# A row mean over 512 MiB: the first tile loaded in four DMAs over strided partitions

## The chip, the cores and the metric

The kernel runs on one core of a Trainium2 chip, alone. The metric is the device time of one launch in microseconds; lower is better. The core has TensorE (PE), VectorE (DVE), ScalarE (ACT), GpSimd (POOL) and SyncE (SP), and 16 DMA engines that move data between HBM and the on-chip memory, SBUF. SBUF has 128 partitions; a tile has rows in partitions.

## The reference

```python
def setup_inputs():
    return {"x": np.random.randn(64, 256, 8192).astype(np.float32)}

def reference(x):
    return np.mean(x, axis=2)
```

The input is 64 x 256 = 16,384 rows of L = 8192 float32 numbers, 536.87 MB in all. Each row gives one number, its mean, so the output is 65.5 kB.

## The kernel before

The rows are taken in tiles of 256: partition p of a tile holds rows 2p and 2p + 1 of it, one after the other, so that it is 16,384 numbers, or 65,536 contiguous bytes of HBM, for each partition. `NP` = 63 tiles go this way (t = 0 to 62), and the last 256 rows go as two half tiles of 128 rows, one row to a partition; the second of these is cut into four column chunks, so that little work is left after the last bytes have landed.

Three buffers (`NBUF` = 3) of 128 x 16,384 float32 take the tiles in turn; tile t goes to buffer t mod 3. Each buffer has its own semaphore, `in_sems[t % NBUF]`, which a DMA raises by 16 when all of its parts have landed.

- SP issues all loads in order (`sync_program`, lines 91 to 101). From tile 3 on it first waits until VectorE has done the tile that was in the buffer before (`dve_sem`). After the loads it issues the three stores of the output.
- VectorE (`vector_program`) waits for a tile's semaphore and sums each of the two rows of each partition with one `tensor_reduce` (line 119). For tile t the semaphore has to stand at 16 for each tile that the buffer has taken, this one among them: `16 * (t // NBUF + 1)`.
- ScalarE (`scalar_program`) is idle until the end, where it shares the last full tile and the half tiles with VectorE (line 153).
- At the end TensorE transposes the sums, so that they can be stored as contiguous rows, and ScalarE scales them by 1/L. The very last 128 rows are summed up and transposed on VectorE (lines 143 to 147).
- GpSimd writes an identity matrix and zeros at the start (lines 76 to 79).

The order of work is written by hand, in each engine's program. One thing is done after that: the instructions of the first `NBUF` loads, which wait for nothing, are cut out of the program and put ahead of SP's first drain, which belongs to a barrier of all engines at the start (lines 192 to 200). SP thus issues these loads before it comes to the barrier. The code counts them: it takes the first `NBUF` instructions that follow the position `first`.

Of the kernel before, what the change touches and what calls it, by code (L numbers as in the profile page):

```python
# [6 lines left out]
def bass_global_avg_pool_1d_kernel(  # L7
# [4 lines left out]
    P = 128  # L12
# [13 lines left out]
    NP = rows // (R * P) - 1  # L26
    NBUF = 3
# [5 lines left out]
    x_pair = x_rows.rearrange("(t p r) l -> t p (r l)", p=P, r=R)  # L33
# [8 lines left out]
    with ExitStack() as ctx:  # L42
        E = ctx.enter_context
        bufs = [E(nc.sbuf_tensor(f"buf{i}", [P, R * L], f32)) for i in range(NBUF)]
        res = E(nc.sbuf_tensor("res", [P, NP, R], f32))
        res1 = E(nc.sbuf_tensor("res1", [P, 2], f32))
        part = E(nc.sbuf_tensor("part", [P, 8], f32))
        fin = E(nc.sbuf_tensor("fin", [P, 32], f32))
        fint = E(nc.sbuf_tensor("fint", [P, 32], f32))
        ident = E(nc.sbuf_tensor("ident", [P, P], f32))  # L50
        outsb = E(nc.sbuf_tensor("outsb", [NP, P, R], f32))
        out1sb = E(nc.sbuf_tensor("out1sb", [1, P], f32))
        ps = [E(nc.psum_tensor(f"ps{r}", [NP, P], f32)) for r in range(R)]
        psone = E(nc.psum_tensor("psone", [1, P], f32))

        in_sems = [E(nc.semaphore(f"in_sem{i}")) for i in range(NBUF)]
        one_sem = E(nc.semaphore("one_sem"))
        ch_sems = [E(nc.semaphore(f"ch_sem{i}")) for i in range(NCH)]
        dve_sem = E(nc.semaphore("dve_sem"))
        act_sem = E(nc.semaphore("act_sem"))  # L60
        prep_sem = E(nc.semaphore("prep_sem"))
        pe_sem = E(nc.semaphore("pe_sem"))
        cp_sem = E(nc.semaphore("cp_sem"))
        fin_sem = E(nc.semaphore("fin_sem"))
        out_sems = [E(nc.semaphore(f"out_sem{i}")) for i in range(3)]

        b1 = NP % NBUF
        b2 = (NP + 1) % NBUF
        buf1 = bufs[b1]
        buf2 = bufs[b2]  # L70
        offs = [sum(CH[:i]) for i in range(NCH)]
        s0 = CH[0] // 2 - L // 64
        s1 = CH[1] // 2

        def gpsimd_program(eng):
            eng.memset(fin[:], 0.0).then_inc(prep_sem, 1)  # L76
            eng.memset(ident[:], 0.0).then_inc(prep_sem, 1)  # L77
            eng.wait_ge(prep_sem, 2)
            eng.affine_select(  # L79
                out=ident[:],  # L80
                in_=ident[:],
                compare_op=mybir.AluOpType.not_equal,
                fill=1.0,
                base=0,
                pattern=[[-1, P]],
                channel_multiplier=1,
            ).then_inc(prep_sem, 1)

        first = len(nc.main_func.blocks[0].instructions)

        def sync_program(eng):
            for t in range(NP):
                if t >= NBUF:
                    eng.wait_ge(dve_sem, t - NBUF + 1)
                eng.dma_start(bufs[t % NBUF][:], x_pair[t]).then_inc(in_sems[t % NBUF], 16)  # L95
            eng.wait_ge(dve_sem, NP - NBUF + 1)
            eng.dma_start(buf1[:, :L], x_one[T1]).then_inc(one_sem, 16)
            eng.wait_ge(dve_sem, NP - NBUF + 2)
            for c in range(NCH):
                sl = slice(offs[c], offs[c] + CH[c])  # L100
                eng.dma_start(buf2[:, sl], x_one[T2][:, sl]).then_inc(ch_sems[c], 16)  # L101

            eng.wait_ge(cp_sem, 2)
            eng.dma_start(out_pair[0:NP, :], outsb[:].rearrange("t p r -> t (p r)")).then_inc(
                out_sems[0], 16
            )
            eng.wait_ge(cp_sem, 3)
            eng.dma_start(out_one[T1 : T1 + 1, :], out1sb[:]).then_inc(out_sems[1], 16)
            eng.wait_ge(fin_sem, 3)
            eng.dma_start(out_q[4 * T2 : 4 * T2 + 4, :], fint[0:P:32, :]).then_inc(  # L110
                out_sems[2], 16
            )
            for s in out_sems:
                eng.wait_ge(s, 16)

        def vector_program(eng):
            for t in range(NP - 1):
                eng.wait_ge(in_sems[t % NBUF], 16 * (t // NBUF + 1))
                eng.tensor_reduce(  # L119
                    res[:, t, :],  # L120
                    bufs[t % NBUF][:].rearrange("p (r l) -> p r l", r=R),
                    X,
                    ADD,
                ).then_inc(dve_sem, 1)
            t = NP - 1
            eng.wait_ge(in_sems[t % NBUF], 16 * (t // NBUF + 1))
            eng.tensor_reduce(res[:, t, 0:1], bufs[t % NBUF][:, :L], X, ADD).then_inc(dve_sem, 1)  # L127
            eng.wait_ge(one_sem, 16)
            eng.tensor_reduce(res1[:, 0:1], buf1[:, : L // 2], X, ADD).then_inc(dve_sem, 1)  # L129
            eng.wait_ge(ch_sems[0], 16)  # L130
            eng.tensor_reduce(part[:, 0:1], buf2[:, :s0], X, ADD).then_inc(dve_sem, 1)  # L131
            eng.wait_ge(ch_sems[1], 16)
            eng.tensor_reduce(  # L133
                part[:, 1:2], buf2[:, offs[1] : offs[1] + s1], X, ADD
            ).then_inc(dve_sem, 1)
            eng.wait_ge(ch_sems[3], 16)
            eng.tensor_reduce(  # L137
                part[:, 2:3], buf2[:, offs[3] : offs[3] + CH[3]], X, ADD
            ).then_inc(dve_sem, 1)
            eng.wait_ge(dve_sem, NP + 4)  # L140
            eng.wait_ge(act_sem, 5)
            eng.wait_ge(prep_sem, 1)
            eng.tensor_reduce(fin[:, 0:1], part[:, 0:6], X, ADD).then_inc(fin_sem, 1)  # L143
            eng.wait_ge(fin_sem, 1)
            eng.transpose(fint[:], fin[:]).then_inc(fin_sem, 1)  # L145
            eng.wait_ge(fin_sem, 2)
            eng.tensor_scalar(  # L147
                fint[:], fint[:], inv, None, mybir.AluOpType.mult
            ).then_inc(fin_sem, 1)

        def scalar_program(eng):
            def acc(dst, src):
                eng.activation(src, src, Copy, accum_out=dst).then_inc(act_sem, 1)  # L153

            t = NP - 1
            eng.wait_ge(in_sems[t % NBUF], 16 * (t // NBUF + 1))
            acc(res[:, t, 1:2], bufs[t % NBUF][:, L:])
            eng.wait_ge(one_sem, 16)
            acc(res1[:, 1:2], buf1[:, L // 2 : L])

            for r in range(R):
                eng.wait_ge(pe_sem, r + 1)
                eng.activation(outsb[:, :, r], ps[r][:], Copy, scale=inv).then_inc(cp_sem, 1)  # L163
            eng.wait_ge(pe_sem, 3)
            eng.activation(out1sb[:], psone[:], Copy, scale=inv).then_inc(cp_sem, 1)  # L165
            eng.wait_ge(ch_sems[0], 16)
            acc(part[:, 3:4], buf2[:, s0 : CH[0]])
            eng.wait_ge(ch_sems[1], 16)
            acc(part[:, 4:5], buf2[:, offs[1] + s1 : offs[1] + CH[1]])
            eng.wait_ge(ch_sems[2], 16)  # L170
            acc(part[:, 5:6], buf2[:, offs[2] : offs[2] + CH[2]])

        def tensor_program(eng):
            eng.wait_ge(prep_sem, 3)
            eng.wait_ge(dve_sem, NP)
            eng.wait_ge(act_sem, 1)
            for r in range(R):
                eng.transpose(ps[r][:], res[:, :, r], ident[:]).then_inc(pe_sem, 1)  # L178
            eng.wait_ge(dve_sem, NP + 1)
            eng.wait_ge(act_sem, 2)  # L180
            eng.matmul(psone[:], res1[:, 0:1], ident[:], start=True, stop=False)  # L181
            eng.matmul(psone[:], res1[:, 1:2], ident[:], start=False, stop=True).then_inc(pe_sem, 1)  # L182

        sync_program(nc.sync)
        gpsimd_program(nc.gpsimd)
        vector_program(nc.vector)
        scalar_program(nc.scalar)
        tensor_program(nc.tensor)

        stream = nc.main_func.blocks[0].instructions
        loads = stream[first : first + NBUF]
        del stream[first : first + NBUF]
        at = next(
            i
            for i, ins in enumerate(stream)
            if ins.engine == mybir.EngineType.SP and type(ins).__name__ == "InstDrain"
        )
        stream[at:at] = loads  # L200
# [28 lines left out]
```

## Time and profile before

| what | value |
|---|---|
| median of 3 runs | 1247.26 us (1247.18 to 1247.38) |
| the profiled execution | 1247.12 us |
| its span, from the first to the last instruction | 1245.3 us |
| VectorE busy | 1085.6 us, 87% |
| DMA queue q1, share of 16 engines' span | 99.7%, mean 431 GB/s |
| one `tensor_reduce` of a full tile (line 119) | 17.22 us |
| one issue of a load on SP (line 95) | 0.33 to 0.43 us |
| from a load's issue to its landing (line 95) | 21.9 us for the first, 40.8 us median |

The profile is one execution, recorded by the hardware. Times in its views are microseconds from the span's start, means of one instruction are in nanoseconds. A row of the timeline has its start, its duration, engine, line, operation, output and input, and in brackets the idle time of the engine before it with what ended that. "SPq" is SP's queue of DMA issues. The DMA row gives the busy share of the 16 DMA engines in tenths, slice by slice, and the row below it the rate in GB/s. The chain is the work that ended last, followed back from the last instruction. The trace also holds a record of every DMA packet, with its start, duration and bytes, from which single packets are told.

### The profile page before, as it was taken

To read this page: it belongs to the slowest core of one execution; us is meant where nothing else is said; L and a number is where in the kernel's file an instruction comes from. 1 tells how busy PE (TensorE), PEld (TensorE's weight loads), DVE (VectorE), ACT (ScalarE), POOL (GpSimd) and SP (SyncE) were. 2 spreads that over 40 slices of the span, in tenths; PEclk is the share of its full clock that TensorE was granted. 3 is DMA by queue.
4 is the path that set the end of the run, shared out by engine and by line. 5 is a ranking of instruction groups with operands and counts; after the bars stand their busy time and mean duration, and the time that the engine had idled before them with its cause. 6 is when DMAs were issued, how large, how long until landed. Compare 5 with 4: busy or idle time off the path is not lost.

```text
span 1245.3 us, 194 instructions
## 1 busy us (share of the span) xinstructions
PE 1.7 (0%) x6; PEld 0.6 (0%) x6; DVE 1085.6 (87%) x70; ACT 17.2 (1%) x14; POOL 0.8 (0%) x7
## 2 busy tenths in 40 slices
PE   0000000000000000000000000000000000000000
PEld 0000000000000000000000000000000000000000
DVE  2898988988889889898898988989889898898897
ACT  0000000000000000000000000000000000000005
POOL 0000000000000000000000000000000000000000
DMA  9999999999999999999999999999999999999998
GB/s 434 421 425 438 438 438 438 436 421 423 438 438 438 438 438 436 410 434 438 438 438 438 438 432 413 436 438 438 436 438 438 421 423 438 438 438 436 438 438 341
DMA packets 9876, 536.95 MB, mean 431 GB/s; under 512 B 1107, under 2 KB 1171, under 8 KB 1427
## 3 DMA queue, kind: packets, MB, share of 16 engines
q1 hardware_dynamic: 9874, 536.94, 99.7%
q14 instruction: 2, 0.01, 0.0%
HBM read 536.87 MB, written 0.07 MB: 431 GB/s over the span
## 4 chain that ended last, share of the span: by engine, by line
DMA 70%; DVE 29%; SPq 0%; issue 0%
DMA buf<-in_x_dram 70%; DVE res L119 29%; SPq L101 0%; DVE part L137 0%; SPq L95 0%; DVE fint L145 0%; DVE fint L147 0%; DVE fin L143 0%
## 5 line engine op out<-in xcount | busy, mean ns | idle before, releaser
L119 DVE TENSOR_REDUCE res<-buf 128x2 f32<-128x16384 f32 x62 | 1067.6, 17220 | 152.9 <-DMA buf<-in_x_dram 152.9
L153 ACT ACTIVATE buf<-buf 128x1024 f32<-128x1024 f32 (+3 forms) x5 | 15.0, 2994 | 1222.3 <-DMA buf<-in_x_dram 1222.2
L127 DVE TENSOR_REDUCE res<-buf 128x1 f32<-128x8192 f32 x1 | 8.7, 8686 | 2.1 <-DMA buf<-in_x_dram 2.1
L129 DVE TENSOR_REDUCE res<-buf 128x1 f32<-128x4096 f32 x1 | 4.4, 4420 | 1.0 <-DMA buf<-in_x_dram 1.0
L131 DVE TENSOR_REDUCE part<-buf 128x1 f32<-128x2176 f32 x1 | 2.4, 2419 | 1.1 <-DMA buf<-in_x_dram 1.1
L178 PE MATMUL ps<-ident,res 128*63 128x128 f32 x2 | 0.7, 430 | 1231.5 <-DVE res L127 1231.5
L153 ACT ACT_TABLE_LOAD x1 | 1.3, 1283 | 1.8 <-PEq L214 1.8
L133 DVE TENSOR_REDUCE part<-buf 128x1 f32<-128x1024 f32 x1 | 1.2, 1219 | 0.1
L137 DVE TENSOR_REDUCE part<-buf 128x1 f32<-128x512 f32 x1 | 0.7, 687 | 0.7 <-DMA buf<-in_x_dram 0.7
L153 ACT ACTIVATION_READ_ACCUMULATOR buf<-buf 128x1 f32 x5 | 0.9, 186 | 0.0
L178 PEld LDWEIGHTS ps<-ident,res 128*63 128x63 f32 x2 | 0.3, 205 | 1231.4 <-issue 1231.4
L182 PE MATMUL psone<-ident,res 128*1 128x128 f32 x2 | 0.6, 421 | 0.0
L181 PE MATMUL psone<-ident,res 128*1 128x128 f32 x2 | 0.6, 397 | 4.7 <-DVE res L129 4.7
L163 ACT ACTIVATE outsb<-ps 63x128 f32<-63x128 f32 x2 | 0.4, 264 | 0.0
L79 POOL TENSOR_SCALAR_AFFINE_SELECT ident<-ident 128x128 f32<-128x128 f32 x1 | 0.3, 292 | 0.2 <-POOL ident L77 0.2
L165 ACT ACTIVATE out1sb<-psone 1x128 f32<-1x128 f32 x1 | 0.3, 267 | 1.5 <-PE psone L182 1.5
L182 PEld LDWEIGHTS psone<-ident,res 128*1 128x1 f32 x2 | 0.3, 128 | 0.2
L145 DVE STREAM_TRANSPOSE fint<-fin 128x32 f32<-128x32 f32 x1 | 0.2, 212 | 0.0
L147 DVE TENSOR_SCALAR fint<-fint 128x32 f32<-128x32 f32 x1 | 0.2, 181 | 0.0
L77 POOL MEMSET ident<- 128x128 f32 x1 | 0.2, 204 | 0.0
L143 DVE TENSOR_REDUCE fin<-part 128x1 f32<-128x6 f32 x1 | 0.2, 158 | 0.0
L76 POOL MEMSET fin<- 128x32 f32 x1 | 0.1, 125 | 1.3 <-POOLq L214 1.3
(5 smaller groups left out, 0.5 us busy)
## 6 DMA issues: line engine op xcount, KB each, us to landing
buf<-in_x_dram SPq DMA_DIRECT2D x1, 4096.0 KB, 31.1
buf<-in_x_dram SPq DMA_DIRECT2D x1, 2304.0 KB, 17.3
buf<-in_x_dram SPq DMA_DIRECT2D x1, 1024.0 KB, 19.4
buf<-in_x_dram SPq DMA_DIRECT2D x63, 40.8
buf<-in_x_dram SPq DMA_DIRECT2D x1, 512.0 KB, 20.2
buf<-in_x_dram SPq DMA_DIRECT2D x1, 256.0 KB, 20.3
out_dram<-outsb SPq DMA_DIRECT2D x1, 63.0 KB
out_dram<-out1sb SPq DMA_DIRECT2D x1, 0.5 KB
```

Of the source, the lines that this page charges most:

```text
L79: eng.affine_select(out=ident[:], in_=ident[:], compare_op=mybir.AluOpType.not_equal, fill=1.0, base=0, pattern=[[-1, P]], channel_multipl ...
L119: eng.tensor_reduce(res[:, t, :], bufs[t % NBUF][:].rearrange("p (r l) -> p r l", r=R), X, ADD,).then_inc(dve_sem, 1)
L127: eng.tensor_reduce(res[:, t, 0:1], bufs[t % NBUF][:, :L], X, ADD).then_inc(dve_sem, 1)
L129: eng.tensor_reduce(res1[:, 0:1], buf1[:, : L // 2], X, ADD).then_inc(dve_sem, 1)
L131: eng.tensor_reduce(part[:, 0:1], buf2[:, :s0], X, ADD).then_inc(dve_sem, 1)
L133: eng.tensor_reduce(part[:, 1:2], buf2[:, offs[1] : offs[1] + s1], X, ADD).then_inc(dve_sem, 1)
L137: eng.tensor_reduce(part[:, 2:3], buf2[:, offs[3] : offs[3] + CH[3]], X, ADD).then_inc(dve_sem, 1)
L153: eng.activation(src, src, Copy, accum_out=dst).then_inc(act_sem, 1)
L163: eng.activation(outsb[:, :, r], ps[r][:], Copy, scale=inv).then_inc(cp_sem, 1)
L178: eng.transpose(ps[r][:], res[:, :, r], ident[:]).then_inc(pe_sem, 1)
L181: eng.matmul(psone[:], res1[:, 0:1], ident[:], start=True, stop=False)
L182: eng.matmul(psone[:], res1[:, 1:2], ident[:], start=False, stop=True).then_inc(pe_sem, 1)
```

## The change

The load of tile 0 is no longer one DMA over all 128 partitions. Four DMAs take its place, on the same queue and in this order: partitions 0, 8, 16, ... (16 of them), partitions 4, 12, 20, ... (16), partitions 2, 6, 10, ... (32) and the odd partitions (64). Each moves the same 65,536 bytes to each of its partitions as before, from the same place in HBM. All four raise the semaphore of buffer 0 by 16, so a new function `landed(t)` gives the count to wait for: 48 more than before for all tiles of buffer 0. The block of instructions that is moved ahead of SP's drain grows by three. All else is as it was.

```diff
+        def landed(t):
+            return 16 * (t // NBUF + 1 + 3 * (t % NBUF == 0))
+
...
         def sync_program(eng):
-            for t in range(NP):
+
+
+            for p, step in ((0, 8), (4, 8), (2, 4), (1, 2)):
+                eng.dma_start(bufs[0][p:P:step, :], x_pair[0][p:P:step, :]).then_inc(
+                    in_sems[0], 16
+                )
+            for t in range(1, NP):
                 if t >= NBUF:
                     eng.wait_ge(dve_sem, t - NBUF + 1)
                 eng.dma_start(bufs[t % NBUF][:], x_pair[t]).then_inc(in_sems[t % NBUF], 16)
...
             for t in range(NP - 1):
-                eng.wait_ge(in_sems[t % NBUF], 16 * (t // NBUF + 1))
+                eng.wait_ge(in_sems[t % NBUF], landed(t))
...
             t = NP - 1
-            eng.wait_ge(in_sems[t % NBUF], 16 * (t // NBUF + 1))
+            eng.wait_ge(in_sems[t % NBUF], landed(t))
...
-        loads = stream[first : first + NBUF]
-        del stream[first : first + NBUF]
+        loads = stream[first : first + NBUF + 3]
+        del stream[first : first + NBUF + 3]
```

The wait for the last full tile changes in the same way in VectorE's and in ScalarE's program.

More of the change, by code (lines that the diff above doesn't have):

```diff
@@ L155, in scalar_program @@
             t = NP - 1
-            eng.wait_ge(in_sems[t % NBUF], 16 * (t // NBUF + 1))
+            eng.wait_ge(in_sems[t % NBUF], landed(t))
             acc(res[:, t, 1:2], bufs[t % NBUF][:, L:])
```

## The prediction

> **What bounds the kernel now.** I read the page first (engine shares, DMA rows, the chain), then the timeline of the first tiles, the DMA view of the first 22 us, and last the waits of SP's queue. The page gives the engines' busy shares, the DMA queues and the chain that ended last:
>
> ```profile
> PE 1.7 (0%) x6; PEld 0.6 (0%) x6; DVE 1085.6 (87%) x70; ACT 17.2 (1%) x14; POOL 0.8 (0%) x7
> ...
> q1 hardware_dynamic: 9874, 536.94, 99.7%
> ...
> DMA 70%; DVE 29%; SPq 0%; issue 0%
> ...
> L119 DVE TENSOR_REDUCE res<-buf 128x2 f32<-128x16384 f32 x62 | 1067.6, 17220 | 152.9 <-DMA buf<-in_x_dram 152.9
> ```
>
> The loads keep the 16 DMA engines busy for 99.7% of the span. VectorE idles 152.9 us in 62 waits, every one for a load. The 29% of the chain that is DVE is the reduce that frees a buffer just ahead of a load; the timeline shows that this is not a true limit:
>
> ```profile
> 0.00 136.28 SPq L95 DMA_DIRECT2D buf<-in_x_dram  x9
> ...
> 1.75 1.28 ACT L153 ACT_TABLE_LOAD   x1 [1.75 <-PEq L214]
> ...
> 21.95 17.22 DVE L119 TENSOR_REDUCE res<-buf 128x2 f32<-128x16384 f32 x1 [21.95 <-DMA buf<-in_x_dram]
> 41.27 17.22 DVE L119 TENSOR_REDUCE res<-buf 128x2 f32<-128x16384 f32 x1 [2.11 <-DMA buf<-in_x_dram]
> 60.62 17.22 DVE L119 TENSOR_REDUCE res<-buf 128x2 f32<-128x16384 f32 x1 [2.13 <-DMA buf<-in_x_dram]
> ```
>
> Tiles arrive 19.3 to 19.4 us apart and a reduce takes 17.22, so VectorE waits about 2.1 us for each. The load of tile 3 goes out when reduce 0 ends, at 39.17 us, while all of tile 2 is still queued in the DMA engines (it takes about 19 us). The DMA queue never runs dry: time lost in any load is lost at the end, and time gained by VectorE is worth nothing.
>
> The DMA view of the first 22 us, 40 slices of 0.55 us; a packet's bytes are booked where it starts:
>
> ```profile
> DMA  0990000990089000950099000920099008900095
> GB/s 0 715 1192 0 0 0 0 1192 715 0 0 357 1549 0 0 0 1668 238 0 0 715 1192 0 0 0 1787 119 0 0 1311 596 0 0 357 1549 0 0 0 1668 238
> ```
>
> The packets come in waves: all 16 engines start one within two slices, then none for some 1.3 us. The trace's packet records give the detail: 63 tiles in 8064 packets of 65,536 bytes (one row pair, one partition), so 128 packets to a tile, 8 to an engine. The first 16 start between 1.04 and 1.45 us and take 2.85 to 3.41 us; every later one takes 2.42 us, and the engines stay within about 0.5 us of each other. One engine moves 65,536 B / 2.42 us = 27.1 GB/s, sixteen 433 GB/s. Tile 0 has landed at 21.92 us. This lockstep matters below.
>
> [...] The trace agrees with 16 times 27.1 GB/s for a full tile[...]. It shows no load on part of the partitions.
>
> **The change part by part.**
>
> *Removed:* one issue (0.42 us of SP) with 8 packets for each engine. *Added:* four issues with 1 + 1 + 2 + 4 packets, again 8 for each engine, in the same bytes and packet size. Packets alone: 0.
>
> *Issue time:* the first issue takes 0.42 us with 0.05 us to the next, so three more are 3 x 0.47 = 1.4 us of SP. The loads of tiles 1 and 2, behind them in SP's queue, go out by 2.8 instead of 1.35 us, and are needed when tile 0's packets run out, near 21 us. The pieces themselves are issued at 0, 0.47, 0.94 and 1.41 us; each starts about 1.04 us after its issue, so piece two is ready at 1.5 us, when piece one runs to 4.1. No engine runs dry. What is behind SP's drain moves 1.4 us as well: the ACT table load at 1.75, POOL's memsets at 1.76. VectorE is not needed before 21.95, so that is hidden by 18 us or more; without cover it would be 1.4 us.
>
> *Completion:* three more semaphore writes on each engine. A period of 19.35 us holds 8 packets (8 x 2.42 = 19.36) and one such write, so they are too short to see: 0 to 0.05 us in all. The waits for 64, 80 and so on replace those for 16, 32; no new wait is added.
>
> *Start:* piece one asks for a single packet of each engine. The engines' first packets spread over 0.40 us and the issue might shorten from 0.42 to 0.33 us (as later L95 issues take), so a gain of 0 to 0.5 us; I take 0.2.
>
> [...] the trace has no price; bounds from both sides. [...] Low end: the engine is the limit, 0. High end: 8 x 2.42 = 19.36 us. I take the high end[...].
>
> *Where the stall goes:* tile 0 lands at 21.9 + 19.4 = 41.3; tile 1 follows 19.35 us later, and VectorE (17.22) keeps up. The load of tile 3 goes out at about 58.5, when tile 2 still has its 19 us ahead. Everything moves by the same amount, and nothing makes it up, as the DMA queue has no slack.
>
> *Sum:* the profiled execution took 1247.12 us: its span 1245.30 and 1.82 outside. 1247.12 + 19.36 - 0.2 + 0.05 = 1266.3. The median of the runs, 1247.26, is 0.14 higher, so 1266.4.
>
> **The rivals.**
>
> *Conflict in part.* [...] only the first two packets of an engine double: 2 x 2.42 = 4.84, 1247.26 + 4.84 - 0.2 = 1251.9. [...] one or two lost packets on top, about 1250 to 1258. For it: the dealing of strided rows is unknown. Against it: full lockstep in the trace[...].
>
> *No conflict; not slower.* If the engine's own datapath is the 27.1 GB/s[...], every packet stays at 2.42 us and only the start moves: 1247.26 - 0.2 = 1247.1, between 1246.7 and 1247.3. Its place is the packets from 1.0 to 21 us; it decides if packets of the 0::8 piece take about 3.1 us at first and those of 4::8 take 2.42. For it: the same 2.42 us, to some ns, in all packets[...]. [...]
>
> *The change does not do what it says.* A piece on fewer than 16 engines would cost more than the high end[...] and I leave it at a few per cent inside the first case's share.
>
> A clear gain has no room: before the first packet lie 1.04 us, and outside the waves the DMA is never idle; 2.5 us cannot come from there.
>
> **How the numbers follow.** Full conflict 0.45, conflict in part 0.25, no conflict 0.28, an unforeseen gain 0.02. A measurement of this kernel can tell about 0.2%, 2.5 us, from no change. The first two cases are slower by more than that (1251.9 is +0.37%), the third is within: faster 0.02, same 0.28, slower 0.70. The predicted time is that of full conflict, 1266.4; its own range is 1262 (some pairs out of step) to 1267.5. No case can be left out of eight in ten, so the range runs from 1246.7 (no conflict, start gain) to 1267.2.
>
> **What would show it.** Right: the first reduce starts near 41 us, then near 61 and 80 at the old 19.35 spacing; packets before 41 us last about 4.8 us; the rate in that stretch is near 217 GB/s; all reduces still 17.22; VectorE's idle time up by 19.4, all in the first wait. Conflict in part: first reduce at 26 to 33 us. No conflict: first reduce within 21.4 to 22.1. Wrong altogether: a delay in a later tile, or a period other than 19.35 us after the first tile, which nothing above provides for.

## The result and the profile after

The kernel with the first tile in four pieces takes 1251.83 us (median; 1251.77 to 1252.15), the kernel before 1247.22 (1246.54 to 1247.38). The ratio is 1.0039 with an interval of 1.0021 to 1.0056: slower by 4.6 us. That lies inside the range given, but far from the predicted 1266.4; it is within 0.1 us of the rival "conflict in part", 1251.9 (in part by luck, see below). The profiled execution took 1252.15 us with a span of 1250.4.

The page of the kernel after, the lines that answer to those shown of before (queue; line, operation, busy time, mean ns, idle time before it):

```profile
q1 hardware_dynamic: 9922, 536.94, 99.7%
...
L128 DVE TENSOR_REDUCE res<-buf 128x2 f32<-128x16384 f32 x62 | 1067.6, 17220 | 158.0 <-DMA buf<-in_x_dram 158.0
```

The reduces are untouched: 62 of 17.22 us. VectorE's idle time rises from 152.9 to 158.0 us, by 5.1, and the span by the same 5.1. The DMA engines are as busy as before, 99.7%, for a longer time, so a slowed packet counts as busy: from 1 to 11 us they moved 236 GB/s instead of 419, at a DMA share of 1.06 against 1.04 (a packet is booked where it starts, so a stretch can show more than 1). The timeline says where the 5.1 us lie:

```profile
0.00 2.52 SPq L98 DMA_DIRECT2D buf<-in_x_dram  x4
...
2.57 119.57 SPq L104 DMA_DIRECT2D buf<-in_x_dram  x7
4.05 1.28 ACT L162 ACT_TABLE_LOAD   x1 [4.05 <-PEq L223]
...
27.17 17.22 DVE L128 TENSOR_REDUCE res<-buf 128x2 f32<-128x16384 f32 x1 [27.17 <-DMA buf<-in_x_dram]
46.51 17.22 DVE L128 TENSOR_REDUCE res<-buf 128x2 f32<-128x16384 f32 x1 [2.12 <-DMA buf<-in_x_dram]
65.86 17.22 DVE L128 TENSOR_REDUCE res<-buf 128x2 f32<-128x16384 f32 x1 [2.13 <-DMA buf<-in_x_dram]
```

The first reduce starts at 27.17 instead of 21.95 us, 5.2 later. From there on the spacing is the old one, 19.34 and 19.35 us. All of the loss is in tile 0, and at most some 0.1 us of it comes back. The DMA view of the first 22 us (slices of 0.55 us, a packet's bytes booked where it starts) shows it wave by wave:

```profile
DMA  0099000000999000000999000990099002950099
GB/s 0 0 1549 357 0 0 0 0 0 0 477 715 715 0 0 0 0 0 0 477 715 715 0 0 0 1192 715 0 0 477 1430 0 0 119 1549 238 0 0 834 1072
```

The waves stand some nine slices apart for the first two packets of an engine (4.9 us), and then four to five (2.4 us), as before the change. The records of single packets tell more. The table has the median duration over the 16 engines of each engine's n-th packet, in us, for this kernel and those of the experiments (0::8 is partitions 0, 8, 16, ..., and 0:64 is partitions 0 to 63):

| kernel | 1 | 2 | 3 | 4 | 5 | 6 | 7 | 8 | 9 (tile 1) |
|---|---|---|---|---|---|---|---|---|---|
| before | 3.17 | 2.42 | 2.42 | 2.42 | 2.42 | 2.42 | 2.42 | 2.42 | 2.42 |
| after: 0::8, 4::8, 2::4, 1::2 | 4.89 | 4.93 | 2.81 | 2.42 | 2.42 | 2.42 | 2.42 | 2.42 | 2.42 |
| 0::4, 2::4, 1::2 | 3.05 | 2.42 | 2.42 | 2.42 | 2.42 | 2.42 | 2.42 | 2.42 | 2.42 |
| after, rows of HBM in order | 4.76 | 4.91 | 2.93 | 2.42 | 2.42 | 2.42 | 2.42 | 2.42 | 2.42 |
| eight times q::8 | 4.91 | 4.92 | 4.91 | 4.91 | 4.91 | 5.13 | 4.92 | 5.12 | 2.85 |
| 0:64, 64:128 | 4.79 | 5.12 | 5.12 | 5.12 | 4.91 | 5.12 | 5.12 | 5.12 | 2.84 |
| 0:16, 16:32, 32:64, 64:128 | 8.69 | 9.29 | 5.65 | 5.12 | 5.01 | 5.12 | 5.12 | 5.12 | 2.82 |
| 32:96, 0:32, 96:128 | 2.99 | 2.42 | 2.42 | 2.42 | 4.61 | 5.13 | 4.95 | 5.12 | 2.93 |

In the kernel after, the packets of 0::8 and 4::8 take twice as long; those of 2::4 (the third and fourth) and 1::2 (the last four) do not. The third, 2.81, starts from 10.65 us on, when packets of 4::8 are still under way; the last of these ends at 11.95.

### The profile page after: what moved, and what is told of

It is laid out like the page before. It is cut to its first block, busy times and chain, and to the rows that moved or that the text cites. A ratio compares the mean times of both kernels' runs of the same rounds, so it can differ in the third digit from the quotient of the medians.

```text
span 1250.4 us, 197 instructions
## 1 busy us (share of the span) xinstructions
PE 1.7 (0%) x6; PEld 0.6 (0%) x6; DVE 1085.6 (87%) x70; ACT 17.2 (1%) x14; POOL 0.8 (0%) x7
## 3 DMA queue, kind: packets, MB, share of 16 engines
q1 hardware_dynamic: 9922, 536.94, 99.7%
## 4 chain that ended last, share of the span: by engine, by line
DMA 70%; DVE 29%; SPq 0%; issue 0%
DMA buf<-in_x_dram 70%; DVE res L128 29%; SPq L98 0%; SPq L110 0%; DVE part L146 0%; DVE fint L154 0%; DVE fint L156 0%; DVE fin L152 0%
## 5 line engine op out<-in xcount | busy, mean ns | idle before, releaser
L128 DVE TENSOR_REDUCE res<-buf 128x2 f32<-128x16384 f32 x62 | 1067.6, 17220 | 158.0 <-DMA buf<-in_x_dram 158.0
## 6 DMA issues: line engine op xcount, KB each, us to landing
buf<-in_x_dram SPq DMA_DIRECT2D x1, 1024.0 KB, 19.4
```

Source lines behind the costliest of these rows:

```text
L128: eng.tensor_reduce(res[:, t, :], bufs[t % NBUF][:].rearrange("p (r l) -> p r l", r=R), X, ADD,).then_inc(dve_sem, 1)
```

## The experiments

My theory after the result, called P: the time of a packet depends on which partitions its piece writes, and it was doubled in the two 16-partition pieces alone. How long the packets of a piece would take under P is, in each expectation, an estimate of mine. Rivals: a fixed cost of each further strided DMA (S); reads of HBM at a pitch of 8 rows (H); the cold start (C); engines that fell out of step after two packets, in pieces that would all be slowed (O). Each experiment changes the load of tile 0 alone, unless it says otherwise; the count in `landed` and the number of loads that are moved ahead follow the number of pieces. Diffs are against the kernel after, the changed lines alone. Ratios are to the kernel before.

### The two 16-partition pieces joined to one of 32

```diff
-            for p, step in ((0, 8), (4, 8), (2, 4), (1, 2)):
+            for p, step in ((0, 4), (2, 4), (1, 2)):
```

> Tile 0 in three DMAs, 0::4, 2::4 and 1::2, so no DMA with 16 partitions. Theory P[...]: all packets 2.42 us after the first, 1247.2 to 1247.7 us. Theory S (each strided DMA, or each further DMA, costs a fixed 1.2 to 1.5 us): two further DMAs, 1249.6 to 1250.3. Theory O (32 strided partitions conflict too and in the changed kernel the engines only got out of step): packets of 4.8 us in the first piece, 1250 to 1252.

Measured: 1247.14 us, ratio 1.000 (0.9992 to 1.0009). The timeline and the DMA view of its first 22 us:

```profile
0.00 1.84 SPq L98 DMA_DIRECT2D buf<-in_x_dram  x3
...
22.32 17.22 DVE L128 TENSOR_REDUCE res<-buf 128x2 f32<-128x16384 f32 x1 [22.32 <-DMA buf<-in_x_dram]
```

```profile
DMA  0099600595009900990029800990059500990099
GB/s 0 0 1311 357 238 0 0 238 1430 238 0 0 1192 715 0 0 596 1311 0 0 119 1430 357 0 0 1192 715 0 0 238 1430 238 0 0 1311 596 0 0 596 1311
```

The old rhythm is there from the first wave. S falls: two further strided DMAs cost nothing that can be told. O falls too: 0::4 takes 3.05 us for an engine's first packet, where the kernel before took 3.17, and 2.42 from the second on. The whole loss of the change belongs to its splitting of 0::4 in two.

### The destinations of the change, the rows of HBM in order

```diff
-            for p, step in ((0, 8), (4, 8), (2, 4), (1, 2)):
-                eng.dma_start(bufs[0][p:P:step, :], x_pair[0][p:P:step, :]).then_inc(
+            for p, step, row in ((0, 8, 0), (4, 8, 16), (2, 4, 32), (1, 2, 64)):
+                n = P // step
+                eng.dma_start(bufs[0][p:P:step, :], x_pair[0][row : row + n, :]).then_inc(
                     in_sems[0], 16
                 )
```

Here `n` is the number of partitions of the piece and `row` its first row of HBM.

> The changed kernel's four DMAs with the same destination partitions, but the rows of HBM taken in order (rows 0 to 15 of the tile for 0::8, 16 to 31 for 4::8, and so on); the rows of tile 0 thus come out in another order. Theory P[...]: unchanged against the changed kernel, first two packets 4.9 us, 1251.6 to 1252.1. Theory H (reads from HBM at a pitch of 8 rows, 512 KiB, run at half the rate): packets 2.42 us, 1247.2 to 1247.7.

Measured: 1252.12 us, 1.0040 (1.0026 to 1.0055). The first reduce starts as late as with the change:

```profile
27.16 17.22 DVE L129 TENSOR_REDUCE res<-buf 128x2 f32<-128x16384 f32 x1 [27.16 <-DMA buf<-in_x_dram]
```

With another pattern of reads and the same pattern of writes the first two packets still take 4.76 and 4.91 us. H falls: the doubling goes with the partitions that are written, not with the rows that are read.

### Eight pieces of 16 partitions

```diff
-            for p, step in ((0, 8), (4, 8), (2, 4), (1, 2)):
+            for p, step in ((0, 8), (4, 8), (2, 8), (6, 8), (1, 8), (3, 8), (5, 8), (7, 8)):
```

> Tile 0 in eight DMAs of 16 partitions, q::8 for q = 0, 4, 2, 6, 1, 3, 5, 7. Theories P and H: every packet of tile 0 takes twice as long, 8 x 2.42 = 19.4 us more plus some 0.4 for the start, 1266 to 1267. Theory C (the doubling belongs to the cold start, the first two packets of an engine, whatever the pieces): 1251.5 to 1252.5. Out of step after a few packets[...]: between 1252 and 1262.

Measured: 1267.05 us, 1.0161 (1.0145 to 1.0176), 20.0 us over the 1247.06 of its runs of before. The DMA view of the first 22 us has the slow rhythm throughout:

```profile
DMA  0099900000999000000999000000999000000999
GB/s 0 0 1192 477 238 0 0 0 0 0 238 1072 596 0 0 0 0 0 0 238 1072 596 0 0 0 0 0 0 238 1072 596 0 0 0 0 0 0 238 1072 596
```

C falls: all eight packets are doubled, not two, and the eighth, at 5.12 us, is no quicker than the first, at 4.91. Six of the pieces take 4.91 or 4.92 us; the sixth and the eighth, 3::8 and 7::8, take 5.13 and 5.12. What makes that difference is not shown. This is the doubling of every packet that the prediction put on the change itself; it is real, and costs what was worked out, but it takes eight such pieces.

### Two contiguous halves

```diff
-            for p, step in ((0, 8), (4, 8), (2, 4), (1, 2)):
-                eng.dma_start(bufs[0][p:P:step, :], x_pair[0][p:P:step, :]).then_inc(
-                    in_sems[0], 16
-                )
+            for p, q in ((0, 64), (64, 128)):
+                eng.dma_start(bufs[0][p:q, :], x_pair[0][p:q, :]).then_inc(in_sems[0], 16)
```

> Tile 0 in two DMAs over the contiguous halves, partitions 0 to 63 and 64 to 127. Theory P with runs of consecutive rows dealt to an engine[...]: packets 4.84 us, 1266 to 1267. Theory P with rows dealt by their place in the list[...]: packets 9.7 us, 1300 to 1306. Theory H (HBM pitch): packets 2.42 us, 1247.2 to 1247.7.

Measured: 1267.97 us, 1.0168 (1.0153 to 1.0183): a doubled packet, eight times, about 1 us above the expected figure. The first reduce:

```profile
43.31 17.22 DVE L126 TENSOR_REDUCE res<-buf 128x2 f32<-128x16384 f32 x1 [43.31 <-DMA buf<-in_x_dram]
```

The second case of the expectation, packets of 9.7 us, falls, and so does H. The first wave in the DMA view has 16 packets of 65,536 bytes (1192 and 715 GB/s in slices of 0.55 us), so sixteen are under way at once. The packets take 5.12 us in each half after its first, which takes 4.79 and 4.91. Sixteen packets in 5.12 us are 205 GB/s, where sixteen in 2.42 are 433: a little less than half.

### Four column quarters over all partitions

```diff
-            for p, step in ((0, 8), (4, 8), (2, 4), (1, 2)):
-                eng.dma_start(bufs[0][p:P:step, :], x_pair[0][p:P:step, :]).then_inc(
-                    in_sems[0], 16
-                )
+            for c in range(4):
+                sl = slice(c * L // 2, (c + 1) * L // 2)
+                eng.dma_start(bufs[0][:, sl], x_pair[0][:, sl]).then_inc(in_sems[0], 16)
```

> Tile 0 in four DMAs, each over all 128 partitions and a quarter of the columns: four issues and four completions without any piece on part of the partitions. Theory P[...]: 1247.0 to 1247.5 us, 2.42 us for each 64 KiB of an engine. A cost of the number of DMAs in front: 1248 or more.

Measured: 1247.07 us, 1.0001 (0.9993 to 1.0010). Four issues and four completions, with all partitions in each, cost nothing.

### The sizes of the change as contiguous runs

```diff
-            for p, step in ((0, 8), (4, 8), (2, 4), (1, 2)):
-                eng.dma_start(bufs[0][p:P:step, :], x_pair[0][p:P:step, :]).then_inc(
-                    in_sems[0], 16
-                )
+            for p, q in ((0, 16), (16, 32), (32, 64), (64, 128)):
+                eng.dma_start(bufs[0][p:q, :], x_pair[0][p:q, :]).then_inc(in_sems[0], 16)
```

> The changed kernel's sizes, 16, 16, 32 and 64 partitions, as contiguous runs: 0:16, 16:32, 32:64, 64:128. Theory P: [...] the first two DMAs (packets of about 10 us), [...] the others (4.9 to 5.1 us): 2 x 7.6 + 6 x 2.6 = 31 us more, 1277 to 1280. [...]

Measured: 1276.55 us, 1.0238 (1.0222 to 1.0253), a little under the 1277 to 1280 of theory P. The 7.6 and 2.6 us there are what packets of about 10 and 5 us take beyond 2.42, an estimate of mine.

```profile
51.68 17.22 DVE L126 TENSOR_REDUCE res<-buf 128x2 f32<-128x16384 f32 x1 [51.68 <-DMA buf<-in_x_dram]
```

The packets of 0:16 take 8.69 us and those of 16:32 take 9.29, 3.8 times 2.42. Those of 32:64 take 5.65 and 5.12, those of 64:128 take 5.01 and then 5.12, about twice 2.42. So the price is not the same for all pieces on part of the partitions, and the number of partitions does not set it: 16 in a row took 8.69 to 9.29 us a packet where 16 at stride 8 took 4.91 to 5.13, and 32 in a row took 5.12 to 5.65 where 32 at stride 4 took 2.42.

### A run of 64 partitions across the middle

```diff
-            for p, step in ((0, 8), (4, 8), (2, 4), (1, 2)):
-                eng.dma_start(bufs[0][p:P:step, :], x_pair[0][p:P:step, :]).then_inc(
-                    in_sems[0], 16
-                )
+            for p, q in ((32, 96), (0, 32), (96, 128)):
+                eng.dma_start(bufs[0][p:q, :], x_pair[0][p:q, :]).then_inc(in_sems[0], 16)
```

> Tile 0 in three contiguous runs, 32:96 first, then 0:32 and 96:128. Theory P[...]: [...] the first four packets take 2.42 us, the last four 4.9 to 5.1: 4 x 2.6 = 10.4 us more, 1257 to 1258.5. Theory N (any DMA on half of the partitions in one run is halved): 1267 to 1268.

Measured: 1257.53 us, 1.0085 (1.0070 to 1.0100). Its DMA view of the first 22 us changes pace in the middle:

```profile
DMA  0099000090009500590009000000099000000099
GB/s 0 0 1192 715 0 0 0 0 1907 0 0 0 1668 238 0 0 238 1668 0 0 0 1907 0 0 0 0 0 0 0 1072 834 0 0 0 0 0 0 0 238 1668
```

Four waves 2.4 us apart for the 64 partitions from 32 to 95, then 4.6 to 5.1 for each of the four packets of the two outer quarters. In 0:64 the same number of partitions in one run took 4.79 and 5.12 us a packet; here, after the first at 2.99, they take 2.42. N falls. It is which partitions a piece writes that counts, not its size.

### The four pieces at tile 30

```diff
+                if t == 30:
+                    for p, step in ((0, 8), (4, 8), (2, 4), (1, 2)):
+                        eng.dma_start(bufs[0][p:P:step, :], x_pair[t][p:P:step, :]).then_inc(
+                            in_sems[0], 16
+                        )
+                    continue
```

Tile 0 is loaded by one DMA here, as in the kernel before, and the three first loads are moved ahead.

> The kernel before, with tile 30 instead of tile 0 loaded by the four DMAs of the change. Theory P with a DMA queue that has no slack: the same 4.6 to 5.1 us, 1251.5 to 1252.3, with one wait of VectorE some 4.6 us longer before the reduce of tile 30. If the tiles queued ahead hide it in the steady state, or the doubling belongs to the start: 1247.0 to 1247.5.

Measured: 1252.07 us, 1.0042 (1.0027 to 1.0057), 5.1 us. The timeline around it (in brackets VectorE's wait before the reduce; the three reduces are those of tiles 29, 30 and 31):

```profile
561.70 2.51 SPq L100 DMA_DIRECT2D buf<-in_x_dram  x4
...
584.23 17.22 DVE L128 TENSOR_REDUCE res<-buf 128x2 f32<-128x16384 f32 x1 [3.20 <-DMA buf<-in_x_dram]
607.92 17.22 DVE L128 TENSOR_REDUCE res<-buf 128x2 f32<-128x16384 f32 x1 [6.48 <-DMA buf<-in_x_dram]
627.27 17.22 DVE L128 TENSOR_REDUCE res<-buf 128x2 f32<-128x16384 f32 x1 [2.13 <-DMA buf<-in_x_dram]
```

With two tiles loaded or queued ahead the loss is the same within the noise, so it does not depend on the start. I had expected one longer wait; there are two. The usual 2.13 us grow by 1.07 before the reduce of tile 29 and by 4.35 before that of tile 30. The records show where the first of them arises. The last packets of tile 29 are hardly slower, 2.57 us at most, and end by 582.84 us; but the last of the tile's 16 semaphore increments comes at 584.20, 1.36 us later, where it is 0.44 us for tile 31. In between, the first packets of 0::8 were under way, from 581.97 on. Whether the one caused the other, no record shows.

## Why the prediction was wrong

**What bounds the kernel: right.** The loads set the end, VectorE follows, and time lost in a load is lost at the end, at tile 0 (4.6 us) as at tile 30 (5.1).

**0::8 and 4::8: right in size.** 2 x 2.42 = 4.84 us was worked out for a packet, and 4.89 and 4.93 were measured. The doubling was an estimate of mine, as no trace of before has a load on part of the partitions; the runs now show it for these pieces, for all of q::8 (4.91 to 5.13) and for the halves 0:64 and 64:128 (4.79 to 5.12).

**2::4 and 1::2: wrong. This is the step that failed.** The prediction took every packet of tile 0 as doubled, in these two pieces as in the first two, and so charged six packets of an engine with another 2.42 us: 6 x 2.42 = 14.5 us. Measured was 2.42 us for each from the fourth packet on, and 3.05 and 2.42 for 0::4 as the first piece. All pieces tried at stride 4 or 2, and the run 32:96, go at 2.42 us a packet once under way. The prediction's "conflict in part" forecast this outcome: two doubled packets of an engine, and the others as before. That a doubling in 0::8 and 4::8 holds for 2::4 and 1::2 as well was not shown by anything in the trace of before.

What stays open is why a set of partitions goes at the full, the half or about a quarter of the rate. The runs show it piece by piece; the records name no partition of a packet, so they do not show what holds it up.

**The start: wrong in sign, and immaterial.** A gain of 0.2 us was put in. The first packets start at 1.41 to 2.14 us instead of 1.04 to 1.45, 0.4 us later in the mean, behind a longer issue. The issues of tile 0 in the kernel after (duration ns: least, median, most):

```profile
L98 SPq DMA_DIRECT2D buf<-in_x_dram x4: 578/593/628, 0.0 to 1.9; - x4
```

Before, L95's first issues took 413 to 432 ns. Three strided pieces start as late, from 1.35 us, and land tile 0 at 22.32 instead of 21.95 us; still their time is within 0.1% of before. Why the few tenths of the start are not seen in the time, no run shows. In the kernel before not every later packet took 2.42 us, as the prediction read it; 77 took over 2.45, and 15 of the engines end the full tiles between 1220.9 and 1221.5 us and one at 1222.17.

**SP's queue: right that it is hidden.** The load of tile 1 went out at 2.57 us and ACT's table load at 4.05 (it had been 1.75), 2.3 us later rather than the 1.4 worked out. Nothing needed either before 20 us.

**The sum, with what was measured:** by the table, an engine's first three packets took 1.72, 2.51 and 0.39 us longer than before and the others nothing: 4.6 us. With the 0.4 us of the later start that makes 5.0, and tile 0's last packet does end at 26.59 instead of 21.58 us. The medians of the runs differ by 4.6. "Conflict in part" came within 0.1 us of the time partly by luck: it put 2.42 us on each of two packets, where the first cost only 1.72 (an engine's first packet had taken 3.17 before as well) and a third cost 0.39, and it took off 0.2 us at the start. The forecast of 19.4 is what eight doubled packets cost, and eight pieces of 16 partitions did cost 20.0.

## What to carry to other kernels

When a load is cut up by partitions, time the packets of each piece: which partitions it writes can set its rate. In these runs an engine's packets of 65,536 bytes took 2.42 us once under way in pieces at stride 4 or 2 over all partitions and in the run 32:96; they took about twice as long (4.6 to 5.7 us) in pieces of 16 at stride 8, in the halves 0:64 and 64:128 and in the quarters 0:32, 32:64 and 96:128, and 3.6 and 3.8 times as long (8.69 and 9.29) in 0:16 and 16:32. Eight slow packets in a row did not recover (5.12 us in the eighth of q::8). Three pieces at strides 4, 4 and 2, or four column slices, cost nothing that could be told (1247.14 and 1247.07 us against 1247.06 and 1246.96). In a kernel like this one, whose loads are the bound, what a slow piece loses goes straight to the end: 4.6 us in the kernel after, where two packets of an engine are slow, and 20.0 where eight are.

## What the runs showed of the hardware beyond that

- In 0:64 and 64:128 most packets took 5.12 us: sixteen of 65,536 bytes in that time are 205 GB/s. In most pieces of q::8 they took 4.91, which is 214 GB/s, and in a full tile 2.42, 433 GB/s.
- In 16:32 a packet took 9.29 us. The packets of the piece start up to 1.6 us apart, and from the first start to the last end 10.85 us pass, so its sixteen packets moved at 97 to 113 GB/s (over 10.85 and over 9.29 us), about a quarter of the 433 of a full tile.
- The issue of a DMA over part of the partitions took 0.57 to 0.66 us where it was strided, and the first packets started 0.3 to 0.4 us later than before. Of the contiguous runs, 0:16, 16:32 and 32:64 took 0.40 to 0.42, those of 64 partitions 0.58 to 0.66, 0:32 behind 32:96 took 0.58, and 96:128 behind that 0.41. The shape alone does not decide it: tile 1's load over all 128 partitions took 0.61 us behind the change's pieces, and tile 0's 0.42 before. What does is open.
